# Reordering the key products and the second compression in a state space stage

## The chip, the cores and the metric

The kernel runs on one core of a Trainium2 chip. The metric is the device time of one execution in microseconds; for several runs the median is given. A core has a matrix engine (TensorE, "PE" in the profile, with its weight loads as "PEld"), VectorE ("DVE"), ScalarE ("ACT"), GpSimd ("POOL") and SyncE ("SP", which issues most DMAs). Each works through a queue of its own in order, and they wait for each other by semaphores.

## The reference

One layer of a hybrid model on 512 tokens of width 1024, in float32. A normalised input is projected by `w_in`. One branch is a state space mixer, the other an attention with three kinds of keys: compressed blocks, selected blocks and a window. Both are merged, and a convolutional feed-forward and a gated embedding follow. What touches this change, cut:

```python
n1 = rmsnorm(h, g_mix)
z = n1 @ w_in
# state space branch: 32 groups of 16 channels, 64 complex states each
bu = einsum('btgc,gpc->btgp', ug, b_bar)
states = associative_scan(combine, (a_seq, bu))        # x[t] = a * x[t-1] + bu[t]
y = einsum('gcp,btgp->btgc', c, states)                # real part
y = gelu(y + d_skip * uf); y = y * sigmoid(y @ w_glu)
# attention branch: the compressed keys and values
def compress_blocks(k, pe, w1, w2):                    # blocks of 32 tokens, stride 16
    flat = (blocks + pe).reshape(..., 32 * 64)
    return gelu(flat @ w1) @ w2
kc = compress_blocks(k_cmp, pe_k, wk1, wk2); vc = compress_blocks(v_cmp, pe_v, wv1, wv2)
# k_sel and k_win are plain columns of z, used by two more softmax branches
...
h = h + mixed @ w_out; h = h + conv_ffn(rmsnorm(h, g_ffn)); h = h + gate * (p @ w_ple_proj)
return rmsnorm(h, g_final)
```

## The kernel before

Every float32 operand of a large product is split into a high and a low part, so that one projection of 128 columns by 512 tokens takes three products for each of its 8 slices of depth: high by high, high by low, low by high (`mm3`, lines 82 to 84). `wload` brings raw weights in (tile `wr`, three buffers), ScalarE copies the high part (`wh`, line 75), and VectorE or GpSimd takes the low part (`wl`, line 54); `wh` and `wl` have two buffers each. `proj` runs the 24 products into a PSUM bank of the tag "acc", of which there are two.

The program opens with a stage whose order is written by hand (`manual_schedule`): nine `warm` products on a tile of ones, the products of the embedding (`pje`), the row norms (`rx`, spread over the rows by the product `rb`), and the value products (`vps`). Outside such blocks a planner of the framework writes the order of each engine's queue. It takes the order of the program as priority, and starts what is ready by its own simulated times. `issue_after(x)` puts the instructions traced inside it, as far as they are on the engine of `x`, behind `x`.

The state space stage follows the queries (`queries`, tile `QT`). It works in four quarters of the 512 channels, each a generator `ssm_quarter(q)` in two parts:

- The first part builds the tables `z` and `x` (VectorE and GpSimd), copies them into `Z` and `CX` (ScalarE), transposes `Z` (`wbps`, line 798, copied to `WB`) and multiplies with the inputs (`wps`, line 807).
- The second part, the quarter's outputs, rotates `wps` by the tables `tab` and scans it on VectorE (line 852), rotates back into `sr`, and multiplies the short-range tables (`tps`, line 832, copied by ScalarE to `tz`). Then come the outputs `yps`: lines 870 (with `sr`) and 872 (with `tz`), and at last `un` and `yT`.

Around these parts lie other products of TensorE, all into the two "acc" banks:

- `compress_in(i)` projects the columns to be compressed. Half of the result is copied to `FL` by ScalarE and half by VectorE (line 899).
- `compress(i)` multiplies `FL` with the first compression weights (`hps`, line 917, 32 products), then transposes `hT` and runs the second layer (`kps`).
- `keys(br)` projects the keys of the selected blocks (0) or of the window (1), and writes them to `KK`: ScalarE copies a half, VectorE subtracts that copy for the low part.
- `gate_done(i)` runs one of the gate projections.

The order in which the program traces all this is the loop at the end of the functions below: it alternates parts of quarters with `compress_in`, `compress` and `keys`. After this stage come the compressed attention (`compressed`, tile `cs`), the output gate (`glu`), the attention units (`sps`, `ptp`) and the feed-forward (`ua`, `ub`).

Of the kernel before, what the change touches and what calls it, by code (L numbers as in the profile page):

```python
# [9 lines left out]
F32 = mybir.dt.float32  # L10
# [8 lines left out]
P = 128  # L19
T = 512  # L20
NQ = T // P
D = 1024
KD = D // P
# [21 lines left out]
def hybrid_kernel(ctx: ExitStack, tc: tile.TileContext, A, out):  # L45
# [7 lines left out]
    def tt(o, a, b, op, e=V):  # L53
        e.tensor_tensor(o, a, b, op=op)  # L54
# [19 lines left out]
    def copy(o, a):  # L74
        S.activation(o, a, AF.Copy)  # L75
# [126 lines left out]
    def proj(c0, e=V, w=None):  # L202
        hi, lo = w or wload("w_in", INW, 0, c0, KD, P, e)
        ps = bank("acc", "pj")
        for k in range(KD):
            mm3(ps, hi[:, k], lo[:, k], n1h[:, k], n1l[:, k], k == 0, k == KD - 1)
        return ps
# [244 lines left out]
    with tc.manual_schedule(engines={mybir.EngineType.PE, mybir.EngineType.Activation, mybir.EngineType.DVE,  # L452
                                    mybir.EngineType.Pool}):
        warm = bank("s", "warm")
        for _ in range(9):
            PE.matmul(warm[:, :P], heat, heat, start=True, stop=True)
        angled = angles()

        def some(n):
            for _ in range(n):  # L460
                next(angled, None)

        for k in range(2):
            copy(pT[0][:, k], pin[:, k])
            V.tensor_copy(wp[0][:, 0, k], wpr[:, 0, k])
            tt(pT[1][:, k], pin[:, k], pT[0][:, k], SUB)
            tt(wp[0][:, 1, k], wpr[:, 0, k], wp[0][:, 0, k], SUB)
        rho_steps = exp_of(rho, lr, "e1", G)

        def some_rho(n):  # L470
            for _ in range(n):
                next(rho_steps, None)

        for k in range(2):
            for n in range(3):
                for qt in range(NQ):
                    embedded(0, qt, (n,), (k,))
        some(7)
        for k in range(2):
            copy(wp[1][:, 0, k], wpr[:, 1, k])  # L480
            tt(wp[1][:, 1, k], wpr[:, 1, k], wp[1][:, 0, k], SUB)
        some(9)
        k4 = (range(4), range(4, 8))
        squared(0)
        embedded(1, 0)
        rooted(0)
        squared(1)
        spread(0)
        embedded_out(0, 2, V)
        embedded_out(0, 0)  # L490
        embedded_out(0, 1)
        rooted(1)
        some_rho(5)
        embedded(1, 1)
        copy(*wv(0, 0))
        x_scaled(0, 0)
        n_high(0, 0)
        x_scaled(0, 1)
        embedded(1, 2)
        n_high(0, 1)  # L500
        wv_lo(0)
        n_low(0, 0)
        n_low(0, 1)
        spread(1)
        copy(*wv(0, 1))
        wv_lo(1)
        x_scaled(1, 0)
        squared(2)
        embedded_out(1, 0)
        embedded_out(0, 3)  # L510
        n_high(1, 0)
        x_scaled(1, 1)
        n_high(1, 1)
        squared(3)
        rooted(2)
        embedded(1, 3)
        embedded_out(1, 2)
        n_low(1, 0)
        v_pass(0, 0)
        v_pass(0, 1)  # L520
        v_pass(0, 2)
        n_low(1, 1)
        v_pass(1, 0, k4[0])
        spread(2)
        v_pass(1, 0, k4[1])
        x_scaled(2, 0)
        v_pass(1, 2)
        x_scaled(2, 1)
        rooted(3)
        v_pass(1, 1)  # L530
        spread(3)
        x_times_g(3, 1)
        embedded_out(1, 1)
        n_high(2, 0)
        x_scaled(3, 0)
        v_pass(2, 0, k4[0])
        n_high(2, 1)
        v_pass(2, 0, k4[1])
        n_low(2, 0)
        n_low(2, 1)  # L540
        x_scaled(3, 1)
        u_split(0, 0)
        n_high(3, 0)
        n_high(3, 1)
        v_pass(2, 2)
        v_pass(3, 0, k4[0])
        v_pass(2, 1)
        v_pass(3, 2)
        n_low(3, 0)
        n_low(3, 1)  # L550
        v_pass(3, 1)
        v_pass(3, 0, k4[1])
        u_split(0, 1)
        embedded_out(1, 3)
        some_rho(50)
        for qt in range(2):
            v_high(qt)
            v_low(qt)
        some(50)
        trig_at = last(mybir.EngineType.DVE)  # L560
        u_split(1, 0)
        for qt in (2, 3):
            v_high(qt)
            v_low(qt)
        zero_at = last(mybir.EngineType.Activation)
        u_split(1, 1)
# [189 lines left out]
    SR = [pM.tile([P, 4, NCH + 1], F32, name=f"sr{i}") for i in range(2)]  # L756
    for t in SR:
        G.memset(t[:, :, 0:1], 0.0)
    spread_at, so_at, latest = [], [], last
    PZ = [pM.tile([P, NPAIR // 2, 2, L], F32, name=f"PZ{i}") for i in range(2)]  # L760
    for t, x in zip(PZ, (PR, PI)):
        for i in range(2):
# [5 lines left out]
    def ssm_quarter(q):  # L768
# [65 lines left out]
                                  x[:, b, 0:m].rearrange("p j g c -> p (j g c)"), start=s0, stop=s1)  # L834
        tz = mt4("tz")
        copy(tz, tps.rearrange("p (a b) -> p a b", a=4))

        dec = pM.tile([P, 4, HC], F32, name="dec", tag="dec")
        copy(dec, rho4[:, pq, None].to_broadcast([P, 4, HC]))
# [54 lines left out]
    def compress_in(i):  # L894
        ps = proj(OFF_KV + i * P, G)
        for g in range(2):
            for j in range(2):
                x = ps[64 * g:64 * g + 64, j:j + 1]
                (V.tensor_copy if g else copy)(
                    FL[64 * j:64 * j + 64, i, :, g, 0:NCMP - 1],  # L900
                    bass.AP(tensor=x.tensor, offset=x.offset, ap=[x.ap[0], [2, 16], [16, NCMP - 1]]))

    def keys(br):
        ps = proj(OFF_KV + 256 + 256 * br, G)
        for g in range(2):
            s0, o0 = 64 * g, 64 * (1 - g)
            copy(KK[s0:s0 + 64, br, g], ps[s0:s0 + 64])
            tt(KK[o0:o0 + 64, br, g], ps[s0:s0 + 64], KK[s0:s0 + 64, br, g], SUB)

    def compress(i):  # L910
        hps = bank("acc", "hps")
        for c in range(2):
            if c == len(w1s[i]):
                w1s[i].append(w1load("cmp_wv1", 1, pw.tile([P, 8, P], F32, name="w1", tag="wr", bufs=3)))
            for k in range(8):
                r = 64 * (k % 2)
                PE.matmul(hps[r:r + 64, P:2 * P], FL[:, i, 8 * c + k].rearrange("p g n -> p (g n)"), w1s[i][c][:, k],
                          start=c == 0 and k < 2, stop=c == 1 and k >= 6)
        hT = pw.tile([P, P], F32, name="hT", tag="mg")
        copy(hT, hps[:, P:2 * P])  # L920
        for x in range(2):
            PE.matmul(hps[:, 0:64], hT, ident[:, 64 * x:64 * x + 64], start=x == 0, stop=x == 1)
        kps = bank("so"[1 - i], "kps")
        h1 = slot(pa, "hid", [P, 64], F32, f"hid{i}")
        pe = small("pe", 1, 2)
        if i == 0:
            with tc.issue_after(spread_at[2]):
                S.activation(small("pe", 1, 2), rowok, AF.Gelu_apprx_tanh)
        copy(pe, hps[:, NCMP - 1:NCMP])
        S.activation(h1, hps[:, 0:64], AF.Gelu_apprx_tanh, bias=pe)  # L930
        if i == 0:
            PE.matmul(kps[:, 0:64], W2[:, 0:2].rearrange("p a d -> p (a d)"), h1, start=True, stop=True)
            kv = kps[:, 0:64].rearrange("p (g n) -> p g n", g=2)
            for s in range(2):
                r = slice(64 * s, 64 * s + 64)
                split(KC[r, 0, :, 32 * s:32 * s + 32], KC[r, 1, :, 32 * s:32 * s + 32], kv[r])
            return None
        VC = slot(pa, "v4", [P, 2, 4, 2, HD], F32R, "VC")
        hid = pw.tile([P, 2, 4, NCMP], F32, name="hidv", tag="mg")
        V.tensor_copy(hid, h1.rearrange("p (g n) -> p g n", g=2)[:, :, None].to_broadcast([P, 2, 4, NCMP]))  # L940
        for g in range(2):
            PE.matmul(kps[:, 64 * g:64 * g + 64], hid[:, g].rearrange("p r n -> p (r n)"), W2[:, 2],
                      start=True, stop=True)
            vc = pw.tile([P, 4, HD], F32, name="vc", tag="mg")
            tt(vc, kps[:, None, 64 * g:64 * g + 64].to_broadcast([P, 4, HD]),
               blk[:, :, None].to_broadcast([P, 4, HD]), MUL)
            split(VC[:, g, :, 0], VC[:, g, :, 1], vc)
        return VC


    t1s = []
# [17 lines left out]

    quarters = [ssm_quarter(q) for q in range(4)]  # L970
    next(quarters[0])
    for q in range(4):
        if q < 3:
            next(quarters[q + 1])
        next(quarters[q])
        if q == 0:
            compress_in(0)
            compress_in(1)
        elif q == 1:
            compress(0)  # L980
            keys(0)
            t1s.append(slot(py, "t8", [P, 4, T], F32, "t1a"))
        elif q == 2:
            VC = compress(1)
            keys(1)
            gate_done(0)
    sM.close()
    sS.close()
    PTC = slot(pa, "ptc", [P, 2, 2, T], F32R, "PTC")
# [1278 lines left out]
```

## Time and profile before

| | us |
|---|---|
| median of 3 runs | 781.89 (781.85 to 782.31) |
| the profiled execution | 782.55 |
| its span, first to last instruction | 780.8 |
| TensorE busy | 767.2 |
| VectorE busy | 612.1 |
| ScalarE busy | 434.6 |
| GpSimd busy | 232.5 |

The profile holds one execution. Its span is what the rows count from, and the execution's own time is 1.75 us longer. A row of the order of time has a start, a length, the engine, the line of the source, the operation, the tile written and the tiles read, and in brackets how long the engine had been idle and what it waited for. A row "x8" merges eight instructions, from the first start to the last end. A product of TensorE overlaps its successor, so that two rows overlap too; the pace is read from the starts.

### The profile page before, as it was taken

To read this page: it belongs to the slowest core of one execution; us is meant where nothing else is said; L and a number is where in the kernel's file an instruction comes from. 1 tells how busy PE (TensorE), PEld (TensorE's weight loads), DVE (VectorE), ACT (ScalarE), POOL (GpSimd) and SP (SyncE) were. 2 spreads that over 40 slices of the span, in tenths; PEclk is the share of its full clock that TensorE was granted. 3 is DMA by queue.
4 is the path that set the end of the run, shared out by engine and by line. 5 is a ranking of instruction groups with operands and counts; after the bars stand their busy time and mean duration, and the time that the engine had idled before them with its cause. 6 is when DMAs were issued, how large, how long until landed. Compare 5 with 4: busy or idle time off the path is not lost.

```text
span 780.8 us, 12274 instructions
## 1 busy us (share of the span) xinstructions
PE 767.2 (98%) x4362; PEld 647.0 (83%) x4362; DVE 612.1 (78%) x1194; ACT 434.6 (56%) x775; POOL 232.5 (30%) x264
## 2 busy tenths in 40 slices
PE   9999999999999999999999999999999999999995
PEld 8888878888888888888998888888888888888884
DVE  7997999775677739799758888888987677779486
ACT  6835645656676746444554454554444456645664
POOL 4667532126554535000031222213222110000123
PEclk9999999999999999999999999999999999999998
DMA  9954131423324318210355877867888456658762
GB/s 359 359 161 147 59 96 43 123 81 95 95 69 117 127 49 314 81 55 1 108 217 175 310 276 265 294 243 263 321 271 257 154 209 249 227 189 325 266 245 109
DMA packets 51932, 144.53 MB, mean 185 GB/s; under 512 B 6176, under 2 KB 8352, under 8 KB 51872
## 3 DMA queue, kind: packets, MB, share of 16 engines
q1 hardware_dynamic: 51008, 142.18, 52.9%
q10 hardware_dynamic: 864, 1.57, 0.5%
q8 instruction: 34, 0.56, 0.3%
q14 instruction: 26, 0.21, 0.1%
HBM read 112.28 MB, written 27.26 MB: 179 GB/s over the span
## 4 chain that ended last, share of the span: by engine, by line
PE 90%; DVE 6%; issue 1%; ACT 1%; DMA 1%; SPq 0%; POOLq 0%; ACTq 0%; POOL 0%
PE pj L82 6%; PE pj L83 6%; PE pj L84 6%; PE ua L1664 5%; PE ua L1665 5%; PE ub L1665 5%; PE ua L1670 5%; PE ub L1664 5%; PE ub L1670 5%; PE p L84 4%; PE p L82 4%; PE p L83 4%; PE sps L1089 2%; PE ptp L1109 2%; PE br L82 2%; PE br L84 2%
## 5 line engine op out<-in xcount | busy, mean ns | idle before, releaser
L54 POOL TENSOR_TENSOR wl<-wr,wh 128x1024 fp32r<-128x1024 f32 x45 | 114.1, 2536 | 315.2 <-ACT wh L75 185.9
L75 ACT ACTIVATE wh<-wr 128x1024 fp32r<-128x1024 f32 x96 | 100.7, 1050 | 60.4 <-issue 19.8
L82 PE MATMUL pj<-n1h,wh 128*128 128x512 f32 x224 | 90.8, 406 | 0.3 <-DVE QT L54 0.3
L83 PE MATMUL pj<-n1l,wh 128*128 128x512 f32 x224 | 87.9, 392 | 0.0
L84 PE MATMUL pj<-n1h,wl 128*128 128x512 f32 x224 | 87.8, 392 | 0.0
L54 DVE TENSOR_TENSOR wl<-wr,wh 128x1024 fp32r<-128x1024 f32 (+1 forms) x51 | 62.1, 1218 | 18.0 <-ACT wh L75 17.9
L1664 PE MATMUL ua<-n2h,wh 128*128 128x512 f32 x160 | 62.4, 390 | 0.0
L1665 PE MATMUL ua<-n2l,wh 128*128 128x512 f32 x160 | 62.3, 389 | 0.0
L1664 PE MATMUL ub<-n2h,wh 128*128 128x512 f32 x160 | 62.2, 389 | 0.0
L1665 PE MATMUL ub<-n2l,wh 128*128 128x512 f32 x160 | 62.2, 389 | 0.0
L63 DVE SCALAR_TENSOR_TENSOR cv<-ua,cols,cv 128x511 f32<-128x511 f32 (+1 forms) x44 | 33.0, 749 | 23.5 <-ACT cv L1511 22.7
L84 PEld LDWEIGHTS pj<-n1h,wl 128*128 128x128 f32 x224 | 42.1, 188 | 8.8
L82 PEld LDWEIGHTS pj<-n1h,wh 128*128 128x128 f32 x224 | 42.2, 188 | 8.2 <-DVE QT L54 0.8
L83 PEld LDWEIGHTS pj<-n1l,wh 128*128 128x128 f32 x224 | 42.2, 188 | 7.5 <-issue 0.2
L63 DVE SCALAR_TENSOR_TENSOR cv<-ub,cols,cv 128x511 f32<-128x511 f32 (+1 forms) x44 | 32.9, 748 | 15.7 <-ACT cv L1511 14.8
L60 POOL TENSOR_SCALAR pr<-pr,su,gates 128x512 f32<-128x512 f32 (+2 forms) x64 | 38.6, 617 | 16.6 <-DVE su L1101 15.7
L75 ACT ACTIVATE ph<-ptp 128x128 fp32r<-128x128 f32 (+1 forms) x64 | 27.8, 435 | 26.2 <-PE ptp L1109 26.0
L54 DVE TENSOR_TENSOR pl<-ptp,ph 128x128 fp32r<-128x128 f32 (+1 forms) x64 | 31.0, 486 | 14.0 <-ACT ph L75 13.0
L1670 PE MATMUL ua<-n2h,wl 128*128 128x512 f32 x160 | 39.5, 389 | 0.0
L1670 PE MATMUL ub<-n2h,wl 128*128 128x512 f32 x160 | 39.5, 389 | 0.0
L75 ACT ACTIVATE ffa<-cv 128x256 fp32r<-128x256 f32 x22 | 9.2, 418 | 52.7 <-DVE cv L54 48.6
L1100 ACT ACTIVATE pr<-pr,nb 128x512 f32<-128x512 f32 (+2 forms) x64 | 35.5, 558 | 3.0 <-DVE nb L1098 2.9
(523 smaller groups left out, 2091.2 us busy)
## 6 DMA issues: line engine op xcount, KB each, us to landing
wr<-in_w_up_dram SPq DMA_DIRECT2D x44, 512.0 KB, 4.4
wr<-in_w_in_dram SPq DMA_DIRECT2D x28, 512.0 KB, 3.9
b<-in_w_down_dram SPq DMA_DIRECT2D x22, 512.0 KB, 5.6
bs<-b SPq DMA_DIRECT2D x44, 256.0 KB, 5.5
ue<-bs SPq DMA_DIRECT2D x21, 512.0 KB, 4.8
wr<-in_w_down_dram SPq DMA_DIRECT2D x11, 512.0 KB, 5.4
gs<-gph SPq DMA_DIRECT2D x10, 512.0 KB, 6.0
gs<-gpl SPq DMA_DIRECT2D x10, 512.0 KB, 6.8
```

The costliest lines, as they stand in the source:

```text
L54: e.tensor_tensor(o, a, b, op=op)
L60: e.tensor_scalar(o, a, s1, s2, op0=op0, op1=op1)
L63: e.scalar_tensor_tensor(o, a, s, b, op0=op0, op1=op1)
L75: S.activation(o, a, AF.Copy)
L82: PE.matmul(ps, lh, rh, start=start, stop=False, skip_group_check=goes_on)
L83: PE.matmul(ps, lh, rl, start=False, stop=False, skip_group_check=goes_on)
L84: PE.matmul(ps, ll, rh, start=False, stop=stop, skip_group_check=goes_on)
L1089: PE.matmul(o, self.QQ[:, x, qt * P:(qt + 1) * P], KK[:, :, self.g, :w] if both else KK[:, self.br, self.g, :w], start=x == 0, stop=x == 1)
L1100: S.activation(pp, pp, AF.Exp, bias=nb, scale=-1.0, accum_out=su)
L1664: PE.matmul(ps, hi[:, k], n2h[:, k], start=k == 0, stop=False)
L1665: PE.matmul(ps, hi[:, k], n2l[:, k], start=False, stop=False)
L1670: PE.matmul(ps, lo[:, k], n2h[:, k], start=False, stop=k == KD - 1)
```

## The change

Nine `warm` products become eight. `keys` becomes a generator: it first runs the sixteen products with the high weights, with a stop after the first eight, then the eight with the low weights, then the copies to `KK`, which are put behind the copy of `tz` of quarter 1 (for keys(0)) or quarter 2 (for keys(1)) on ScalarE. `compress` gets a stop after its `hps`. The loop is written out: both `compress_in`, the `hps` of compress(0) and the first eight products of keys(0) are traced before quarter 0's outputs, which are put behind these eight on TensorE, as is the rest of compress(0). The remaining products of keys(0) and the `hps` of compress(1) come before quarter 1's outputs.

```diff
--- before.py
+++ after.py
@@ -452,7 +452,7 @@
     with tc.manual_schedule(engines={mybir.EngineType.PE, mybir.EngineType.Activation, mybir.EngineType.DVE,
                                     mybir.EngineType.Pool}):
         warm = bank("s", "warm")
-        for _ in range(9):
+        for _ in range(8):
             PE.matmul(warm[:, :P], heat, heat, start=True, stop=True)
         angled = angles()
 
@@ -756,7 +756,7 @@
     SR = [pM.tile([P, 4, NCH + 1], F32, name=f"sr{i}") for i in range(2)]
     for t in SR:
         G.memset(t[:, :, 0:1], 0.0)
-    spread_at, so_at, latest = [], [], last
+    spread_at, so_at, tz_at, latest = [], [], [], last
     PZ = [pM.tile([P, NPAIR // 2, 2, L], F32, name=f"PZ{i}") for i in range(2)]
     for t, x in zip(PZ, (PR, PI)):
         for i in range(2):
@@ -834,6 +834,7 @@
                                   x[:, b, 0:m].rearrange("p j g c -> p (j g c)"), start=s0, stop=s1)
         tz = mt4("tz")
         copy(tz, tps.rearrange("p (a b) -> p a b", a=4))
+        tz_at.append(latest(mybir.EngineType.Activation))
 
         dec = pM.tile([P, 4, HC], F32, name="dec", tag="dec")
         copy(dec, rho4[:, pq, None].to_broadcast([P, 4, HC]))
@@ -901,11 +902,22 @@
                     bass.AP(tensor=x.tensor, offset=x.offset, ap=[x.ap[0], [2, 16], [16, NCMP - 1]]))
 
     def keys(br):
-        ps = proj(OFF_KV + 256 + 256 * br, G)
+        hi, lo = wload("w_in", INW, 0, OFF_KV + 256 + 256 * br, KD, P, G)
+        ps = bank("acc", "pj")
+        for k in range(KD):
+            PE.matmul(ps, hi[:, k], n1h[:, k], start=k == 0, stop=False)
+            PE.matmul(ps, hi[:, k], n1l[:, k], start=False, stop=False)
+            if k == 3:
+                yield
+        for k in range(KD):
+            PE.matmul(ps, lo[:, k], n1h[:, k], start=False, stop=k == KD - 1)
+        yield
         for g in range(2):
             s0, o0 = 64 * g, 64 * (1 - g)
-            copy(KK[s0:s0 + 64, br, g], ps[s0:s0 + 64])
+            with tc.issue_after(tz_at[br + 1]):
+                copy(KK[s0:s0 + 64, br, g], ps[s0:s0 + 64])
             tt(KK[o0:o0 + 64, br, g], ps[s0:s0 + 64], KK[s0:s0 + 64, br, g], SUB)
+        yield
 
     def compress(i):
         hps = bank("acc", "hps")
@@ -916,6 +928,7 @@
                 r = 64 * (k % 2)
                 PE.matmul(hps[r:r + 64, P:2 * P], FL[:, i, 8 * c + k].rearrange("p g n -> p (g n)"), w1s[i][c][:, k],
                           start=c == 0 and k < 2, stop=c == 1 and k >= 6)
+        yield
         hT = pw.tile([P, P], F32, name="hT", tag="mg")
         copy(hT, hps[:, P:2 * P])
         for x in range(2):
@@ -934,7 +947,8 @@
             for s in range(2):
                 r = slice(64 * s, 64 * s + 64)
                 split(KC[r, 0, :, 32 * s:32 * s + 32], KC[r, 1, :, 32 * s:32 * s + 32], kv[r])
-            return None
+            yield
+            return
         VC = slot(pa, "v4", [P, 2, 4, 2, HD], F32R, "VC")
         hid = pw.tile([P, 2, 4, NCMP], F32, name="hidv", tag="mg")
         V.tensor_copy(hid, h1.rearrange("p (g n) -> p g n", g=2)[:, :, None].to_broadcast([P, 2, 4, NCMP]))
@@ -945,7 +959,7 @@
             tt(vc, kps[:, None, 64 * g:64 * g + 64].to_broadcast([P, 4, HD]),
                blk[:, :, None].to_broadcast([P, 4, HD]), MUL)
             split(VC[:, g, :, 0], VC[:, g, :, 1], vc)
-        return VC
+        yield VC
 
 
     t1s = []
@@ -969,21 +983,31 @@
 
     quarters = [ssm_quarter(q) for q in range(4)]
     next(quarters[0])
-    for q in range(4):
-        if q < 3:
-            next(quarters[q + 1])
-        next(quarters[q])
-        if q == 0:
-            compress_in(0)
-            compress_in(1)
-        elif q == 1:
-            compress(0)
-            keys(0)
-            t1s.append(slot(py, "t8", [P, 4, T], F32, "t1a"))
-        elif q == 2:
-            VC = compress(1)
-            keys(1)
-            gate_done(0)
+    next(quarters[1])
+    compress_in(0)
+    compress_in(1)
+    compressing = [compress(i) for i in range(2)]
+    keyed = [keys(br) for br in range(2)]
+    next(compressing[0])
+    next(keyed[0])
+    high_at = latest(mybir.EngineType.PE)
+    with tc.issue_after(high_at):
+        next(quarters[0])
+    next(quarters[2])
+    with tc.issue_after(high_at):
+        next(compressing[0])
+    next(keyed[0])
+    next(compressing[1])
+    next(quarters[1])
+    next(keyed[0])
+    t1s.append(slot(py, "t8", [P, 4, T], F32, "t1a"))
+    next(quarters[3])
+    next(quarters[2])
+    VC = next(compressing[1])
+    for _ in keyed[1]:
+        pass
+    gate_done(0)
+    next(quarters[3])
     sM.close()
     sS.close()
     PTC = slot(pa, "ptc", [P, 2, 2, T], F32R, "PTC")
```

## Prediction

> **What bounds the kernel now.** I read the page first, then the waits of TensorE, then the order of time of TensorE, VectorE, ScalarE and GpSimd in the state space stage, and last the start.
>
> ```profile
> span 780.8 us, 12274 instructions
> PE 767.2 (98%) x4362; PEld 647.0 (83%) x4362; DVE 612.1 (78%) x1194; ACT 434.6 (56%) x775; POOL 232.5 (30%) x264
> ...
> PE yps L870 <- DVE sr L54: 1.9, 2, 1.2
> PE warm L456 <- DVE heat L241: 1.1, 1, 1.1
> PE yps L872 <- ACT tz L75: 0.8, 1, 0.8
> PE pj L82 <- DVE QT L54: 0.3, 1, 0.3
> PE vps L300 <- ACT n1h L75: 0.2, 1, 0.2
> ```
>
> TensorE is busy for 98% of the span. The five wait rows are all the waiting it does: 4.3 us in the whole span. So the time is the work of TensorE plus its waits plus what comes before and after it. This change removes one `warm` product and otherwise reorders; apart from what it costs to switch between kinds of products, only the waits can shrink. It aims at the two `yps` rows: 1.9 and 0.8 us, 2.7 us together. That caps the gain, and 0.2% of 782 us, about what a measurement of this kernel can tell from no change, is 1.56 us.
>
> Where these waits lie is seen in TensorE's order of time (start, length, then in brackets the idle time before):
>
> ```profile
> 91.43 1.38 PE L832 MATMUL tps<-CX,Z 128*32 128x128 f32 x64
> 92.74 0.50 PE L83 MATMUL pj<-n1l,wh 128*128 128x512 f32 x1
> 93.08 0.40 PE L84 MATMUL pj<-n1h,wl 128*128 128x512 f32 x1
> 93.40 1.96 PE L917 MATMUL hps<-wk,FL 128*64 128x128 f32 x30
> ...
> 97.85 0.43 PE L870 MATMUL yps<-sr,CX 128*32 128x128 f32 x8 [1.18 <-DVE sr L54]
> ...
> 101.76 0.48 PE L82 MATMUL pj<-n1h,wh 128*128 128x512 f32 x1
> 102.07 0.40 PE L83 MATMUL pj<-n1l,wh 128*128 128x512 f32 x1
> 107.58 0.39 PE L84 MATMUL pj<-n1h,wl 128*128 128x512 f32 x1
> 107.90 0.88 PE L917 MATMUL hps<-wv1c,FL 128*64 128x128 f32 x12
> 109.80 1.38 PE L832 MATMUL tps<-CX,Z 128*32 128x128 f32 x64
> 112.15 0.43 PE L870 MATMUL yps<-sr,CX 128*32 128x128 f32 x8 [0.76 <-DVE sr L54]
> 112.87 0.44 PE L917 MATMUL hps<-wv1c,FL 128*64 128x128 f32 x4
> 113.14 1.04 PE L917 MATMUL hps<-w,FL 128*64 128x128 f32 x16
> 114.98 0.42 PE L872 MATMUL yps<-Uc,tz 128*32 128x128 f32 x8 [0.80 <-ACT tz L75]
> 117.31 0.66 PE L798 MATMUL wbps<-ident,Z 128*128 128x128 f32 x4
> 118.16 0.48 PE L82 MATMUL pj<-n1h,wh 128*128 128x512 f32 x1
> ```
>
> The first wait (1.18 us) stands in quarter 0's outputs, the other two (0.76 and 0.80 us) in quarter 1's. The `pj` from 101.76 to 107.58 are keys(0); the last two `pj` at 92.74 and 93.08 end compress_in(1). The two smallest rows of the waits are of the queries and the value products, before all this. After 114.98 TensorE does not wait any more, so 2 us won here should reach the end. What TensorE waited for stands on the other queues:
>
> ```profile
> 97.12 0.67 DVE L54 TENSOR_TENSOR sr<-f,wps 128x512 f32<-128x512 f32 x1
> 98.77 1.37 DVE L899 COPY FL<-pj 64x496 f32<-64x496 f32 x2
> 111.43 0.67 DVE L54 TENSOR_TENSOR sr<-f,wps 128x512 f32<-128x512 f32 x1
> 114.77 0.69 DVE L54 TENSOR_TENSOR KK<-pj,KK 64x512 fp32r<-64x512 f32 x1
> ...
> 95.23 1.15 ACT L75 ACTIVATE FL<-pj 64x496 f32<-64x496 f32 x2
> 112.85 0.59 ACT L75 ACTIVATE KK<-pj 64x512 fp32r<-64x512 f32 x1 [3.15 <-DVE KK L54]
> 113.46 0.84 ACT L75 ACTIVATE Z<-z 64x256 f32<-64x256 f32 x2
> 114.33 0.60 ACT L75 ACTIVATE tz<-tps 128x512 f32<-128x512 f32 x1
> ...
> 84.17 2.40 POOL L54 TENSOR_TENSOR wl<-wr,wh 128x1024 fp32r<-128x1024 f32 x1
> ```
>
> Three things are to be seen. First, keys(0) had its weights early: the third split on GpSimd, after the two for the compress inputs, ends at 86.57. It started only at 101.76 because its PSUM bank (two of tag "acc") was held by compress_in(1) until VectorE's `FL` copies ended at 100.14, though their `pj` was done at 93.48. So at 96.67 TensorE had almost nothing else to do. Second, VectorE's last `sr` of a quarter ends at 97.79 and at 112.10, and TensorE's `yps` follow at once. Third, `tz` of quarter 1 was copied at 114.33 although its `tps` ended at 111.18: ScalarE stood 3.15 us on a key copy that waited for VectorE, and `tz` was queued behind it and a `Z`.
>
> **Quarter 0: first half of the key products ahead.** The edit traces the compress inputs, `hps` of compress(0) and eight products of keys(0) before quarter 0's outputs, and puts all of that quarter's `tps` and `yps` behind the eighth. What a product costs:
>
> ```profile
> 410.94 1.81 PE ua L1670 x8
> ```
>
> Eight products of this shape take 1.81 us. TensorE, which stood ready at 96.67 (97.85 less 1.18), now arrives at 98.48. To have the bank, VectorE must copy `FL` of compress_in(1) before it ends quarter 0. That is 1.37 us pushed ahead of `sr`, which ends at 97.79 + 1.37 = 99.16. So 0.68 us of wait is left, unless the rest of keys(0), sixteen products that now have bank and weights, is planned into it. The bounds are 0 and 0.68; I take 0.3, near the middle, since the trace cannot show the new order. This term is -1.18 + 0.3 = -0.88.
>
> The start of the eight products has to be checked too, for everything is queued behind them. Without `tps` in front (91.43 to 92.74, 1.31 us) the `pj` ends at 92.17; VectorE's two copies can end at 93.54, ScalarE's at 93.32. TensorE is busy with `hps` (32 products; 30 take 1.89 us) to about 94.1. There is thus half a microsecond of slack, and after it every microsecond that VectorE is late is waited for. `tz` itself comes later, but is not needed before 99.
>
> **Quarter 1: second compression ahead.** All 32 `hps` of compress(1) are now traced before quarter 1's outputs. Twenty of them ran behind the wait: from 112.87 to the end of the second row at 114.18, 1.31 us. TensorE stood ready for `yps` at 111.39 (112.15 less 0.76). It comes 0.88 earlier from quarter 0 and 1.31 later with these products: 111.82, against `sr` at 112.10. VectorE's work before that `sr` is the same in both orders, and the window below shows it full, so I leave its time.
>
> ```profile
> 107.00:118.00 11.00, 9.45 (x214) 7.75 (x212) 10.88 (x20) 4.83 (x11) 3.99 (x4) 1.00 0.30 98
> ```
>
> VectorE (third pair) is busy for 10.88 of these 11 us, TensorE (first) for 9.45. So 0.28 us of the 0.76 is left; bounds 0 and 0.76. Term: -0.48.
>
> **Key copies behind tz.** With quarter 1's `tz` ahead of the copies, ScalarE can copy it after `tps`: 111.18 + 0.60 = 111.78, before `sr`. Term -0.80; with a `Z` (0.84 us) still ahead it would be 112.62 and the wait some 0.2, the other bound being the old 0.80. What waits instead is the bank of keys(0), which keys(1) takes next: its last reader was VectorE's `KK` copy, ending at 115.46. keys(1) would be reached at 118.16 less 2.0, 116.2. So the copies may be 0.7 us later than now at no cost; each microsecond more is a wait before keys(1), unless other work is ready. Behind the waiting copies on ScalarE stand the next `Z` and `WB` copies, for quarter 3, which has slack.
>
> **One more cut in the key products.** From the rows: the first `pj` after another kind starts its successor 0.31 later (101.76 to 102.07), and the last one 0.32 (107.58 to 107.90), where 0.23 is normal. A cut costs 0.17 us; I take one, bounds none and three (0 to 0.5). The order of high and low halves inside a projection is free: the eight above run only low halves and take 0.226 each, like the mixed ones.
>
> **DMA, SP and GpSimd.** One `un` load per quarter is moved behind the keys' weight load on SP; it is needed only after `yps`. The weight loads and GpSimd's splits keep their order among themselves; the second `cmp_wv1` half and the keys' raw weights sit in the same ring of three as before. I cost this at nothing; its cover is that all these weights lay ready long before use (86.57 against 101.76).
>
> **Eight warm products.**
>
> ```profile
> 1.10 4.21 PE L456 MATMUL warm<-heat 128*128 128x128 f32 x18 [1.10 <-DVE heat L241]
> 4.12 0.43 DVE L465 CAST wp<-wpr 128x512 fp32r<-128x512 f32 x1 [3.07 <-DMA wpr<-in_w_ple_proj_dram]
> 5.96 0.81 PE L435 MATMUL pje<-wp,pT 128*128 128x512 f32 x2
> 6.38 0.86 PE L435 MATMUL pje<-wp,pT 128*128 128x512 f32 x3
> 12.04 0.57 POOL L54 TENSOR_TENSOR rx<-rx,expo 128x1 f32<-128x1 f32 x1
> 12.66 0.49 PE L331 MATMUL rb<-root,rx 128*128 128x128 f32 x2
> ```
>
> One `warm` is two of these 18 instructions, which take 4.21 us, so some 0.4 us. The `pje` behind them could then start at 4.55 at the earliest, when VectorE's cast ends. But the row-scale product `rb` at 12.66 waits for GpSimd's `rx`, which ends at 12.61 whatever TensorE does. So the 0.4 us is lost in front of `rb`: term 0. The rows also show TensorE's pace: two starts 0.42 us apart before 6.38, then three products in 0.86, which is the later pace of 0.23. If one product less moved that step, TensorE would be late at `rb`. A step 3 us later would mean 3 us at 0.42 instead of 0.23, or 1.4 us. I take 0 for the term, with bounds 0 and +1.4. [...]
>
> **Sum.** -0.88 - 0.48 - 0.80 + 0.17 + 0 = -1.99 us. The profiled execution took 782.55 us (span 780.8), 0.66 above the median of the runs, 781.89. So 780.56 against its own time, and 779.9 as a median.
>
> **Rivals.**
> - *Part of the waits returns.* The planner orders by its own times, and the trace shows it off by 1.18 us at the first `yps`. If `yps` is again put ahead of the rest of keys(0), if `KK` copies come late for keys(1), or if there are more cuts, then 0.68 + 0.5 instead of 0.3 + 0.17, and 0.4 at `tz` or before keys(1), leave a gain of 0.9: 781.0. For it: VectorE is full, so its work is only moved. Against it: sixteen products lie ready as filler.
> - *Slower: the eight products wait for `FL`.* If VectorE's copies of compress_in(1) stay where they were, ending at 100.14, the eight products cannot start and `tps` and `yps` stand behind them. TensorE runs dry at about 94.7 (`hps`, then a `wbps` group of some 0.6, by the row at 117.31) and waits 5.4 us in place of 1.18, +4.2; quarter 1's waits go (-1.56), the cut costs 0.17: +2.8, 784.7. It turns into a loss when `FL` ends later than about 97.3. Against it: the copies are now traced ahead of quarter 0's outputs, where before they stood behind them. [...]
> - *The clock step moves* (+1.4 at the start): 781.3. Against it, TensorE has work without a gap from 1.10.
>
> **How the numbers follow.** Waits go as summed: 0.54, between 779.0 and 780.3. Part returns: 0.30, between 780.3 and 782.5. The clock: 0.03. Slower by `FL`: 0.13. So faster 0.54, same 0.33, slower 0.13. The range 779.0 to 783.0 leaves out the `FL` case and a little below.
>
> **What would show it.** Right: no idle bracket over 0.4 us before `yps` in either quarter; `tz` of quarter 1 right behind its `tps`; VectorE's second `FL` pair before the last `sr` of quarter 0; eight `pj` before the first `tps`; `rb` still at 12.66. Wrong: a wait of a `pj` for `FL`, a `pj` waiting for `KK`, a first `rb` later than 12.7, or a `yps` still waiting for `sr` by over 1 us.

## The result, and the profile after

The changed kernel takes 789.87 us (median of four runs, 789.54 to 790.39) against 781.87 us before: a ratio of 1.0098, with a 95% interval of 1.0086 to 1.0110. It is 8.0 us slower; 779.9 was forecast.

The page and TensorE's waits of the profiled execution after:

```profile
span 788.2 us, 12268 instructions
PE 769.5 (98%) x4360; PEld 649.2 (82%) x4360; DVE 614.5 (78%) x1194; ACT 435.1 (55%) x775; POOL 233.4 (30%) x264
...
PE pj L908 <- DVE FL L900: 5.5, 1, 5.5
PE pct L1043 <- DVE cmps L54: 1.1, 1, 1.1
PE warm L456 <- DVE heat L241: 1.1, 1, 1.1
PE yps L871 <- DVE sr L54: 0.7, 1, 0.7
PE pj L82 <- DVE QT L54: 0.5, 1, 0.5
PE yps L873 <- ACT tz L75: 0.4, 1, 0.4
PE vps L300 <- ACT n1h L75: 0.2, 1, 0.2
```

The share of busy time is again 98%, and says nothing. The sums say more: the waits add up to 9.5 us where they were 4.3, and TensorE is busy for 2.3 us longer although it has two instructions fewer. Together that is 7.5 us, and the span grew by 7.4. So there are two questions: where the waits come from, and why the same products take longer. TensorE's order of time answers the second:

```profile
91.12 1.97 PE L929 MATMUL hps<-wk,FL 128*64 128x128 f32 x32
98.54 0.77 PE L908 MATMUL pj<-n1h,wh 128*128 128x512 f32 x1 [5.46 <-DVE FL L900]
99.11 0.63 PE L909 MATMUL pj<-n1l,wh 128*128 128x512 f32 x1
99.53 0.63 PE L908 MATMUL pj<-n1h,wh 128*128 128x512 f32 x1
...
102.22 2.36 PE L832 MATMUL tps<-CX,Z 128*32 128x128 f32 x64
...
120.56 0.42 PE L873 MATMUL yps<-Uc,tz 128*32 128x128 f32 x8 [0.36 <-ACT tz L75]
```

TensorE ends the `hps` of compress(0) at 93.09 and then stands for 5.46 us at the first of the eight key products. Behind the wait these products start 0.43 apart instead of 0.23, and the 64 `tps` take 2.36 us instead of 1.38. The table of stretches shows the granted clock (third number from the right; first pair TensorE, third VectorE):

```profile
93.10:96.00 2.90, 0.00 (x0) 0.00 (x0) 2.90 (x6) 0.69 (x2) 1.78 (x1) 1.00 0.08 11
...
98.50:100.00 1.50, 1.46 (x4) 1.20 (x5) 1.50 (x3) 0.00 (x0) 0.00 (x0) 0.50 0.00 0
...
102.00:104.00 2.00, 2.00 (x55) 1.78 (x58) 2.00 (x4) 0.42 (x1) 0.10 (x1) 0.50 0.00 0
104.00:105.00 1.00, 1.00 (x34) 0.82 (x26) 1.00 (x3) 0.48 (x2) 0.00 (x0) 0.69 0.00 0
```

The clock fell to half during the wait, at about 97.8, and stayed there until about 104.6. VectorE was not idle meanwhile: it is busy for all of 93.10 to 96.00. What it did, and when ScalarE was done with its half of the same copies:

```profile
93.35 0.68 DVE L54 TENSOR_TENSOR sr<-f,wps 128x512 f32<-128x512 f32 x1
93.94 0.69 DVE L54 TENSOR_TENSOR f<-wps,tab 128x512 f32<-128x512 f32 x1
...
95.74 0.69 DVE L54 TENSOR_TENSOR wps<-wps,tab 128x512 f32<-128x512 f32 x1
96.33 0.68 DVE L54 TENSOR_TENSOR sr<-f,wps 128x512 f32<-128x512 f32 x1
97.03 1.37 DVE L900 COPY FL<-pj 64x496 f32<-64x496 f32 x2
...
111.36 1.28 DVE L54 TENSOR_TENSOR sr<-f,wps 128x512 f32<-128x512 f32 x2 [2.84 <-PE yps L871]
...
92.36 1.15 ACT L75 ACTIVATE FL<-pj 64x496 f32<-64x496 f32 x2
```

VectorE's `FL` copies still stand behind quarter 0's last `sr`, and between the two `sr` lie four instructions of quarter 1's rotation (93.94 to 96.33). The eight products need the bank those copies release, and everything of quarter 0's outputs now stands behind the eight. The last `sr` row is the other side: having been waited for, VectorE runs dry itself, 2.84 us before quarter 1's `sr`, because its buffer was held by quarter 0's late `yps`.

### The profile page after: what moved, and what is told of

Its sections match the earlier page's. It is cut to its first block, busy times and chain, and to the rows that moved or that the text cites. A ratio compares the mean times of both kernels' runs of the same rounds, so it can differ in the third digit from the quotient of the medians.

```text
span 788.2 us, 12268 instructions
## 1 busy us (share of the span) xinstructions
PE 769.5 (98%) x4360; PEld 649.2 (82%) x4360; DVE 614.5 (78%) x1194; ACT 435.1 (55%) x775; POOL 233.4 (30%) x264
## 4 chain that ended last, share of the span: by engine, by line
PE 90%; DVE 6%; ACT 1%; issue 1%; DMA 1%; SPq 0%; POOLq 0%; ACTq 0%; POOL 0%
PE pj L82 5%; PE pj L83 5%; PE pj L84 5%; PE ua L1688 5%; PE ua L1689 5%; PE ub L1689 5%; PE ub L1694 5%; PE ua L1694 5%; PE ub L1688 5%; PE p L83 4%; PE p L82 4%; PE p L84 4%; PE sps L1113 2%; PE ptp L1133 2%; PE br L82 2%; PE br L83 2%
## 5 line engine op out<-in xcount | busy, mean ns | idle before, releaser
L82 PE MATMUL pj<-n1h,wh 128*128 128x512 f32 x208 | 84.6, 407 | 0.5 <-DVE QT L54 0.5
L83 PE MATMUL pj<-n1l,wh 128*128 128x512 f32 x208 | 81.6, 392 | 0.0
L84 PE MATMUL pj<-n1h,wl 128*128 128x512 f32 x208 | 81.3, 392 | 0.0
L84 PEld LDWEIGHTS pj<-n1h,wl 128*128 128x128 f32 x208 | 39.1, 188 | 8.2
L82 PEld LDWEIGHTS pj<-n1h,wh 128*128 128x128 f32 x208 | 39.1, 188 | 7.8 <-DVE QT L54 0.9
L83 PEld LDWEIGHTS pj<-n1l,wh 128*128 128x128 f32 x208 | 39.2, 189 | 6.5
```

The source lines that it names most:

```text
L82: PE.matmul(ps, lh, rh, start=start, stop=False, skip_group_check=goes_on)
L83: PE.matmul(ps, lh, rl, start=False, stop=False, skip_group_check=goes_on)
L84: PE.matmul(ps, ll, rh, start=False, stop=stop, skip_group_check=goes_on)
```

## The experiments

"The lock" is the part that traces the eight products early and puts quarter 0's outputs behind them.

| kernel | median, us | the traced execution, us | ratio to before (95%) |
|---|---|---|---|
| changed kernel | 789.87 | 789.97 | 1.0086 to 1.0110 |
| eight warm products alone | 782.26 | 781.79 | 0.9991 to 1.0008 |
| key copies behind tz alone | 782.56 | 782.56 | 0.9995 to 1.0013 |
| second compression ahead alone | 788.27 | 787.55 | 1.0070 to 1.0096 |
| the lock alone | 787.27 | 787.30 | 1.0051 to 1.0078 |
| changed, without the two edges of the lock | 783.04 | 783.01 | 0.9999 to 1.0018 |
| changed, the wait filled with products | 788.19 | 788.27 | 1.0061 to 1.0092 |
| changed, FL ahead of quarter 1's rotation | 787.06 | 788.73 | 1.0051 to 1.0077 |
| changed, FL ahead of quarter 0's rotation back | 784.32 | 783.62 | 1.0015 to 1.0034 |
| changed, FL all on ScalarE | 784.83 | 784.95 | 1.0020 to 1.0045 |
| before, FL all on ScalarE | 786.35 | 784.62 | 1.0031 to 1.0057 |
| before, both sr first | 784.19 | 784.59 | 1.0017 to 1.0034 |
| before, both sr and FL first | 786.35 | 787.27 | 1.0042 to 1.0072 |

The kernel before ran at medians of 782.24 to 782.30 beside these. None of the thirteen is faster than it. In five of them the executions lie 2 to 4 us apart: the second compression alone (787.55 to 790.59), `FL` ahead of quarter 1's rotation (786.01 to 788.73), and the last three rows (784.62 to 786.50, 783.27 to 785.89, 784.88 to 789.22). A trace explains its own execution there, and not the median.

**The parts, one by one: the lock.** The changed kernel with nine warm products, the old key copies, and compress(1) traced where it was:

```diff
-    next(compressing[1])
     next(quarters[1])
...
-            with tc.issue_after(tz_at[br + 1]):
-                copy(KK[s0:s0 + 64, br, g], ps[s0:s0 + 64])
+            copy(KK[s0:s0 + 64, br, g], ps[s0:s0 + 64])
```

> The changed kernel with the other three parts taken back: nine warm products, the key copies to KK where they were, and hps of compress(1) behind quarter 1's outputs. What is left is the eight key products ahead of quarter 0's outputs with these locked behind them. Theory (this part alone makes the loss): a wait of a pj for FL of 5.2 to 5.7 us, half pace behind it, 789.0 to 790.5. Rival (the parts lose only together): under 786.

```profile
98.24 0.77 PE L908 MATMUL pj<-n1h,wh 128*128 128x512 f32 x1 [5.45 <-DVE FL L900]
```

787.27 us. The same wait is there, to 0.01 us, so the lock alone makes 5.0 of the 8.0 us. The expectation that it makes all of it was wrong: 3.0 us belong to the rest (2.6 between the two medians; the kernel before stood 0.4 higher in that comparison). With the lock in place, whether compress(1) is traced early or not changes no queue: the program has the same instructions in the same order on all five engines. What is left between this kernel and the changed one is the key copies and one warm product, which by itself measures nothing (next run).

**Eight warm products** (`range(9)` to `range(8)`):

> The kernel before with eight warm products in place of nine, nothing else. Theory (the row-scale product rb waits for GpSimd's rx, which hangs on a DMA): no change, 781.9 within 0.3, unless the DMA lands so early that TensorE is the later of the two (then up to -0.2). Rival 1: the 0.8 us by which the changed kernel's profile is ahead at the queries came from the missing warm product: 781.1. Rival 2: the step of TensorE's pace moves by some microseconds: +1.4, 783.3.

782.26 against 782.30. Nothing, as forecast.

**Key copies behind tz**, the other parts left out:

```diff
+            with tc.issue_after(tz_at[br + 1]):
+                copy(KK[s0:s0 + 64, br, g], ps[s0:s0 + 64])
```

> The kernel before with one part of the change alone: the KK copies behind tz on ScalarE. Theory: the 0.80 us wait of yps for tz in quarter 1 goes and nothing takes its place: 781.1 (780.8 to 781.5), tz of quarter 1 within 0.2 us of the end of its tps. Rival (keys(1) then waits for its bank, or yps waits for sr by as much): 781.9, with a pj row waiting for KK.

```profile
118.19 0.50 PE L82 MATMUL pj<-n1h,wh 128*128 128x512 f32 x1 [1.05 <-DVE KK L54]
```

The wait of 0.80 for `tz` is gone, and keys(1) now waits 1.05 for its bank. A swap. Under the lock the same edit is dearer. VectorE's four `KK` copies, as the view of one tile groups them, in the changed kernel and in the lock alone:

```profile
L54 DVE TENSOR_TENSOR KK<-pj,KK x4: 684/689/694, 122.1 to 145.9; 64x512 fp32r<-64x512 f32 x4
```
```profile
L54 DVE TENSOR_TENSOR KK<-pj,KK x4: 685/689/693, 109.6 to 131.2; 64x512 fp32r<-64x512 f32 x4
```

With the lock alone the first two fill VectorE's idle stretch ahead of quarter 1's `sr`. Tied to `tz` the four move 11 to 15 us later, and the last of them into work with little room: from 140 to 160 us VectorE is busy for 19.02 us in the changed kernel, for 17.42 with the lock alone. There TensorE waits for it, 0.71 us at quarter 3's `sr` and 1.12 at `cmps`; with the lock alone it waits at neither. Together with 0.36 for ScalarE's `tz` at 120.56 that is 2.2 of the 2.6 us between the two spans. The two programs differ in these copies, a warm product and what the planner ordered anew around them; how the copies make each of the waits is read from the traces, not tested.

**Second compression ahead alone**, on the kernel before:

```diff
+        if q == 1:
+            next(compressing[0])
+            next(compressing[0])
+            next(compressing[1])
         next(quarters[q])
```

> The kernel before with only the second compression's first products (hps of compress(1)) traced ahead of quarter 1's outputs. Theory, as in the prediction: quarter 1's wait for sr falls from 0.76 to about 0.3, with more filler in front of it, and the time by about 0.5, to 781.7. Rival: the planner changes the order around it and the wait turns up elsewhere, at tz, KK or a bank: 782.2 to 783.5.

```profile
120.02 0.74 DVE L63 SCALAR_TENSOR_TENSOR un<-un,cols,yps 128x512 f32<-128x512 f32 x1
...
120.90 1.02 PE L798 MATMUL wbps<-ident,Z 128*128 128x128 f32 x4 [3.66 <-DVE un L63]
```

788.27, slower by 6 us. Quarter 1's `yps` are done at 115.29, but the planner put the `un` that empties their bank at 120.02, behind quarter 2's rotation back, and TensorE waited 3.66 us for the bank. The clock is at half behind it (0.50 granted), for 3.4 us from 120.99 on. Both theories fell short: the second said that the wait turns up elsewhere, but named other places and a smaller price.

**Without the edges of the lock.** The changed kernel, with both `issue_after(high_at)` taken away:

```diff
-    with tc.issue_after(high_at):
-        next(quarters[0])
+    next(quarters[0])
```

> The changed kernel without the two edges that put quarter 0's outputs and the rest of compress(0) behind the eighth key product; the order of the program stays. Theory (the copies' late place on VectorE is the cause and the edges only hold tps back; the planner still writes the pj ahead of most of yps): a pj still waits for FL, some 3 to 4.5 us, split by four yps, 785.5 to 789. Rival (the edges are the cause): no pj wait over 1 us and 782 to 783.5.

```profile
94.59 0.43 PE L871 MATMUL yps<-sr,CX 128*32 128x128 f32 x8 [1.08 <-DVE sr L54]
...
96.22 0.50 PE L908 MATMUL pj<-n1h,wh 128*128 128x512 f32 x1 [0.61 <-ACT hid L943]
...
97.47 1.37 DVE L900 COPY FL<-pj 64x496 f32<-64x496 f32 x2
```

783.04: 6.8 us come back, all but about a microsecond. The copies are as late as before (97.47), but the key products do not wait for them: they start at 96.22, ahead of the copies. They take the other "acc" bank, that of compress(0)'s `hps`, which ScalarE's `hid` releases. Under the lock the rest of compress(0) stands behind the eight products, so that bank cannot come free first, and only the one that the late copies hold is left. So the edges do two things: they tie the key products to the late bank, and quarter 0's outputs to the key products. They were not taken away one at a time. TensorE's waits in this trace add up to 3.8 us, half a microsecond less than before the change; but TensorE is busy for 0.9 us longer (768.1), with a stretch at half clock from 96.69 to 100.11, behind the waits of 1.08 and 0.61.

**The wait filled.** 27 products (54 instructions) into an unused part of the `hps` bank, between `hps` and the key products:

```diff
     next(compressing[0])
+    for _ in range(27):
+        PE.matmul(filled[0][:, 256:256 + P], ident, ident, start=True, stop=True)
     next(keyed[0])
```

> The changed kernel with 27 products of the identity, whose results nobody reads, between hps of compress(0) and the eight key products (into unused columns of the hps bank, 54 instructions of some 0.10 us). Theory (after the 5.5 us of idling TensorE runs at half its pace until about 104.5, which costs some 2.8 us: 8 products at 0.43 instead of 0.23, tps in 2.14 instead of 1.31, yps): the FL wait shrinks to under 0.5 us of idle, the products behind it start 0.23 apart, and 787.1 (786.5 to 787.8) where the changed kernel takes 789.9. Rival (the slow stretch costs nothing, since VectorE sets the time there): 789.5 to 790.5, though the pace is back.

```profile
93.32 6.29 PE L996 MATMUL hps<-ident 128*128 128x128 f32 x54
99.37 0.49 PE L908 MATMUL pj<-n1h,wh 128*128 128x512 f32 x1
...
101.41 1.38 PE L832 MATMUL tps<-CX,Z 128*32 128x128 f32 x64
```

788.19, or 1.7 us less than the changed kernel, though the key products start no earlier. The clock stays at 1.00 (from 91 to 118 us), and the key products start 0.23 to 0.24 apart again. So the half clock costs at least 1.7 us here; I had expected more, and some of it went into the filler, which ended later than the wait.

**Why the copies are late.** First, quarter 1's rotation is put behind both `sr` of quarter 0 and behind `FL` (the edit ties the later quarters' rotations to their `sr` too, which changes nothing there). TensorE's order stays that of the changed kernel; on VectorE the planner also places a few `z` steps earlier:

```diff
-        with tc.issue_after(so_at[-1]) if q else nullcontext():
+        with tc.issue_after(so_at[-1]) if q else nullcontext(), tc.issue_after(so_at[-2]) if q else nullcontext(), \
+                tc.issue_after(fl_at[0]) if q else nullcontext():
             for f, w in zip(f4, wps):
...
         tt(so[0], h[0], rr[1], SUB)
+        so_at.append(latest(mybir.EngineType.DVE))
         tt(so[1], h[1], rr[0], ADD)
         so_at.append(latest(mybir.EngineType.DVE))
```

> The changed kernel with one thing added on VectorE alone: the first rotation of quarter 1 (four instructions, f and wps, 2.4 us) is put behind both sr of quarter 0 and behind the FL copies of compress_in(1). TensorE's order is that of the changed kernel, instruction for instruction. In the changed kernel these four stand ahead of the second sr (96.33) and so ahead of FL (97.03 to 98.40). Theory: the copies are late because of what VectorE's queue holds ahead of them. Then FL starts at 97.03 - 2.40 = 94.6 and ends at 96.0, the wait of the first pj falls from 5.46 to about 3.0 us (from 93.1 to 96.1), and the time by 2.4, to 787.4, or, if an idle stretch that short leaves the clock at 1.00, by another 1.7 (the price from the filled wait), to 785.7. Rival: the copies wait for something else (ScalarE's half ends at 93.51, the products at 92.2, so only VectorE's own queue is left, but also the bank of another reader): the wait stays over 4 us and the time at 789 to 790.

```profile
94.18 1.27 DVE L54 TENSOR_TENSOR sr<-f,wps 128x512 f32<-128x512 f32 x2
95.46 1.37 DVE L902 COPY FL<-pj 64x496 f32<-64x496 f32 x2
...
96.98 0.76 PE L910 MATMUL pj<-n1h,wh 128*128 128x512 f32 x1 [3.06 <-DVE FL L902]
```

The wait falls by 2.40 us, what the four instructions take. That shows why the copies are late: VectorE's queue. The median falls by 2.8 to 787.06, but the traced execution only from 789.97 to 788.73, since the clock is at half for 6.8 us here too, from 96.02 on, still in the wait. The four executions are at 786.01, 787.02, 787.10 and 788.73, with a mean granted clock of 0.996, 0.994, 0.994 and 0.993, so both figures of the theory, 787.4 with the half clock and 785.7 without it, were near. Second, in place of that edit, quarter 0's rotation back is put behind `FL`, and with it all that follows on VectorE:

```diff
+        with tc.issue_after(fl_at[0]) if q == 0 else nullcontext():
             for f, w in zip(h, rr):
                 tt(f, w, tb, MUL)
```

> The changed kernel with one edge more: on VectorE quarter 0's rotation back (the f and wps before sr) is put behind the FL copies of compress_in(1). Theory (all of the loss is the 5.46 us for which the eight locked key products wait for these copies, and the slow clock that follows): the pj wait is gone, FL is copied at 91 to 93, no idle over 0.5 us before yps, 780.0 (779.3 to 780.8). Rival (VectorE is full, so work pulled ahead only delays sr, and the locked products lose anyway): a yps wait of 1 us or more and over 783. Rival (the loss sits later, in quarter 3 and the compressed attention): around 788.

```profile
91.40 1.04 ACT L75 ACTIVATE wh<-wr 128x1024 fp32r<-128x1024 f32 x1
92.35 1.15 ACT L75 ACTIVATE FL<-pj 64x496 f32<-64x496 f32 x2
93.53 1.37 DVE L901 COPY FL<-pj 64x496 f32<-64x496 f32 x2 [2.48 <-ACT FL L75]
...
95.05 0.47 PE L909 MATMUL pj<-n1h,wh 128*128 128x512 f32 x1 [1.97 <-DVE FL L901]
```

Even first in line, VectorE's copies wait 2.48 us until ScalarE's are done, which read the other half of the same bank, and 1.97 us of the wait remain. ScalarE's copies have a queue too: their products end at 91.18, but a weight split (`wh`) runs first, and they start at 92.35. 784.32: still slower than before the change, with new waits at `tz` (1.4) and at a `WB` (1.0).

**Can the rest be bought back?** The four `FL` copies of compress_in(1) on ScalarE, in the changed kernel (the weights of keys(1) behind them) and in the kernel before:

```diff
-                (V.tensor_copy if g else copy)(
+                (V.tensor_copy if g and not i else copy)(
```

> The changed kernel with all four FL copies of compress_in(1) on ScalarE (VectorE has none of them), the next weight split of ScalarE behind them. ScalarE's copy takes 0.58, so four end 2.3 us after the pj, at 93.5 on the changed kernel's clock, where hps ends at 93.1. Theory (the FL wait and what follows is the loss, and VectorE's queue is where it comes from): FL wait at most 0.6, no slow pace, VectorE 1.37 us ahead, 780.5 (779.5 to 781.6). Rival (the waits move on: ScalarE's queue now holds up tz and WB as in the run with FL first): 783 to 784.5, with tz and WB rows of over 1 us.

> The kernel before with all four FL copies of compress_in(1) on ScalarE and nothing else. VectorE, full from 83 to 118, has 1.37 us less to do before quarter 1's sr. Theory (VectorE sets quarter 1's sr): that sr ends 1.3 us earlier, the 0.76 us wait goes, 1.18 at quarter 0 stays, 780.8 (780.2 to 781.5). Rival (ScalarE, with 1.15 us more, is late with tz or WB): 781.8 to 782.6 and new rows of ACT tz or WB.

```profile
PE yps L871 <- DVE sr L54: 0.7, 1, 0.7
PE wps L807 <- ACT WB L75: 0.7, 1, 0.7
PE pj L909 <- ACT FL L75: 0.7, 1, 0.7
```
```profile
PE pj L82 <- DVE KK L54: 2.1, 1, 2.1
PE yps L870 <- DVE sr L54: 1.5, 2, 1.2
```

784.83 and 786.35 (the second trace is of an execution of 784.62). In the changed kernel the wait for `FL` shrinks to 0.7 and the others stay or appear; in the kernel before the second `sr` wait halves (0.76 to 0.36) and a wait of 2.1 for `KK` comes.

The last two go at the first wait of the kernel before, whose trace shows four instructions of quarter 1's rotation between quarter 0's two `sr`. They are put behind both `sr` (the edit above without its second line), and in the other behind `FL` too:

> The kernel before, with one thing changed on VectorE: the next quarter's first rotation is put behind both sr of a quarter, not only behind the one that is traced last (in the kernel before the planner runs the sr traced last first, and then 2.4 us of quarter 1's rotation ahead of the other sr, 94.73 to 97.12). Theory: that order is what makes the two yps rows (1.9 us). The second sr of quarter 0 ends at 97.79 - 2.40 = 95.4, ahead of TensorE, which is ready at 96.67: the wait of 1.18 goes. In quarter 1 two such instructions (1.2 us) stand between the two sr: 112.10 becomes 110.9, TensorE is ready at 111.39 - 1.18 = 110.2, so 0 to 0.7 is left of 0.76. Time 782.2 - 1.2 - 0.1 to 0.7 = 780.3 to 780.9. Rival: the waits move on, as in the runs with FL first, with the key copies behind tz and with FL on ScalarE: pj of keys(0) or keys(1) waits for FL or KK by 1 us or more, and the time is 781.8 to 783.

> The same as the run with both sr first, and the FL copies of compress_in(1) are put ahead of quarter 1's first rotation too. FL then ends near 97.4 + 0 to 0.4 less the two z and wps steps, at about 96.8 in place of 100.14, so keys(0) has its bank when TensorE comes to it at about 100. Theory: as in the run with both sr first, 780.3 to 780.9, and if a pj waits for FL there, less by that wait here. Rival: quarter 1's sr comes later by what is put ahead of its rotation (up to 1.4 us), or the waits turn up at KK: 782 to 783.

```profile
94.34 1.27 DVE L54 TENSOR_TENSOR sr<-f,wps 128x512 f32<-128x512 f32 x2
...
PE wps L807 <- ACT pe L75: 1.5, 2, 1.3
PE yps L871 <- DVE un L63: 1.2, 1, 1.2
```

These rows are of the first of the two. Both `sr` now end at 95.61, and both `sr` waits are gone, 1.9 us, as the theory says. The time is 784.19 and not 780.3 to 780.9, with waits at `wps` and `yps` further on; with `FL` ahead too it is 786.35. The waits moved on, as the rivals say, but not to the places they name: the two `pj` wait only 0.3 us each in the first. Their price was too low. The planner's order of TensorE changed in both as well, so they do not test VectorE's order alone.

## Why the prediction was wrong

- **The step that failed** is the check of when the eight products start. It said that VectorE's two `FL` copies "can end at 93.54", and found half a microsecond of slack. In fact they start at 97.03 and end at 98.40. The working looked at when the copies' input was ready and not at what stood in VectorE's queue, though the quoted row of before had them at 98.77 behind `sr`. Tracing them earlier moved them past a `z` step and a step of quarter 1's rotation, about a microsecond, and not past the rotation back, the two `sr` and the four instructions between them. Why the planner left them there, no run shows. Nor did they run beside ScalarE's: in the run with quarter 0's rotation back behind `FL` they waited 2.48 us until those were done, and 1.97 us of TensorE's wait were left with them first in the queue; with all four on ScalarE 0.71 us were left. And the step took the bank as given: it is the lock that leaves the key products no other, as the run without the edges shows.
- **The rival that happened** was given 0.13. Its mechanism is right: TensorE ran dry (93.09), the wait is 5.46 (forecast 5.4), and `FL` ends at 98.40, beyond the 97.3 from which it counted as a loss. It gave +2.8; the lock alone measures +5.0. The waits of the lock alone grow by 2.9 us (4.3 to 7.2), as forecast. The rest is mostly the clock, which the rival left out of its number: TensorE is busy for 1.8 us longer there. 0.50 is granted from 98 to 104 us, and filling the wait in the changed kernel gives 1.7.
- **Quarter 0's wait, -0.88**: the row for `sr` is gone there, with a dearer wait in its place.
- **Quarter 1's wait, -0.48**: it went, but as TensorE came over 5 us late and VectorE waited instead (2.84). The edit named for it does nothing under the lock, and alone costs 6 us. The term was credited to the wrong thing.
- **Key copies, -0.80**: alone, 0.80 becomes 1.05 elsewhere. The bank was named, with 0.7 us of room; but VectorE's last `KK` copy came 2.7 us later (118.13 for 115.46). Under the lock the term is about +2.6, as the first two copies leave VectorE's idle time and the last ones come into its full time.
- **One more cut and eight warm products**: the second measured 0, the value taken. `rb` comes at 12.10 in the changed kernel and not later. The first is too small to be seen here. The step of TensorE's pace to 0.23, at 6.38 before, comes at 5.73 in the changed kernel; the granted clock reads 1.00 from 5 to 7 us in both traces, and TensorE has no gap from 1.10 to 7 in either. No run shows what sets the step, nor the loss of 1.4.
- **"After 114.98 TensorE does not wait any more, so 2 us won here should reach the end"** was not borne out. No edit of the kernel before that took away one of these waits made it faster: others came in their place.

A reason that would fit all these points stands in the windows. From 80 to 125 us of the kernel before:

```profile
80.00:125.00 45.00, 42.26 (x556) 35.89 (x556) 44.51 (x97) 26.20 (x55) 18.01 (x19) 1.00 0.21 66
```

VectorE is busy for 44.51 of 45 us, TensorE for 42.26. So VectorE has next to no room in this stage, and TensorE's waits may be only where that shows; reordering then moves a wait and does not remove it. This is argued, not shown. Taking 1.37 us of copies off VectorE in the kernel before did not make it faster, but there too, as in most of these edits, the planner ordered the rest anew.

## What to carry to other kernels

Before an order is locked behind a product, follow what releases its bank: find the row of that copy on its own engine and ask what stands ahead of it in that queue, not only when its input is ready. Ask also which bank the lock leaves. Read the load from the stage: where a second engine is busy for 99% of it (here 44.51 of 45 us), expect a wait of the first that you remove to come back elsewhere, and price the edit by the engine that is full. And price a wait of TensorE with the half clock that may come with it: here it came with waits of 3.06, 3.66 and 5.46 us and with 1.08 and 0.61 us close together, but not with single ones of 1.92 and 2.05 us, and filling the wait of 5.46 gave 1.7 us back.

## What the runs showed of the chip that I had not expected

The granted clock in steps of 0.2 us (third number from the right), in the run with `FL` ahead of quarter 1's rotation and in the run without the edges:

```profile
96.00:96.20 0.20, 0.00 (x0) 0.00 (x0) 0.19 (x2) 0.00 (x0) 0.00 (x0) 0.55 0.00 0
...
102.80:103.00 0.20, 0.20 (x18) 0.20 (x13) 0.00 (x0) 0.06 (x1) 0.00 (x0) 0.89 0.00 0
```
```profile
96.60:96.80 0.20, 0.20 (x2) 0.14 (x1) 0.20 (x2) 0.00 (x0) 0.00 (x0) 0.73 0.91 205
...
100.00:100.20 0.20, 0.20 (x14) 0.20 (x10) 0.20 (x2) 0.00 (x0) 0.00 (x0) 0.73 0.00 0
```

In the first the half clock lasts from 96.02 to 102.84, or 6.8 us; in the second from 96.69 to 100.11, or 3.4 us. Of the five such stretches read in these steps, those of the changed kernel and of the lock alone last 6.8 us too, and that of the second compression alone 3.4. In the run with the wait of 3.06 us TensorE worked at half clock for 5.9 us, from 96.98 on. And the clock fell in the second run with no wait near it over 1.08 us, though two stood close together (1.08 and 0.61). The length of the longest wait does not tell the cases apart. In the run with both `sr` and `FL` first the clock stayed at 1.00 through and behind a wait of 1.92 us (105 to 113 us), while behind one of 2.09 us, which ended at 140.27, the products from 142.49 to 144.62 start 0.43 apart, the pace of the half clock. A single wait of 2.05 us (the kernel before with `FL` on ScalarE) left the clock at 1.00 (from 107 to 146 us), and behind one of 1.97 (`FL` ahead of quarter 0's rotation back) the products start 0.23 apart. The wait of 1.92:

```profile
108.54 1.16 PE L807 MATMUL wps<-Uc,WB 128*128 128x128 f32 x8 [1.92 <-ACT pe L75]
...
107.00:109.00 2.00, 0.46 (x4) 0.46 (x5) 2.00 (x4) 1.38 (x5) 0.86 (x3) 1.00 0.00 0
```

What decides it, these runs don't show. Nor do they show why executions of one kernel differ, as those with `FL` ahead of quarter 1's rotation do: 786.01 to 788.73 us, at mean granted clocks of 0.996 to 0.993.
